# Mixture-of-experts feed-forward: weight loads with other contraction orders, bf16 transposes of x, and a finer last weight load

## The chip, the core and the metric

The kernel runs on one core of one Trainium2 chip. The metric is the device time of one execution in microseconds (us); lower is better. The core has TensorE (PE: matmuls, and the loads of their stationary operand, shown apart as PEld), VectorE (DVE), ScalarE (ACT), GpSimd (POOL), SyncE (SP) and 16 DMA engines that every queue shares.

## What is computed

```python
n_experts, capacity, hidden, expert_hidden = 8, 256, 512, 2048   # all inputs float32
def reference(x, w1, w2):          # x [8,256,512], w1 [8,512,2048], w2 [8,2048,512]
    h = np.matmul(x, w1)
    h = np.maximum(h, 0)
    return np.matmul(h, w2).astype(np.float32)
```

For each of eight experts a block of 256 tokens goes through two matrix products with a ReLU between them. Each expert has 4.19 MB of float32 in w1 and as much in w2, 0.52 MB of x and 0.52 MB of output: 67.1 MB of weights in all.

## The kernel before

The program is one loop over the experts, unrolled; a tile framework puts in the semaphores, and the instructions of each engine run in the order in which it placed them.

For one expert `e`:

- SP loads x (`x_sbuf`, L59): 128 tokens per half on the partitions, float32, in runs of 2 KB.
- PE transposes x in eight 128x128 float32 pieces (`xpsum`, L65), one PSUM buffer for all; ACT copies each piece to `xT_sbuf` as bf16 (L68) before the next can start.
- POOL loads w1 (`w1_sbuf`, L71) in one DMA that also casts to bf16. Partition `p` of chunk `ko` holds row `ko*128+p`; a row of w1 is one run of 2048 float32, 8 KB, and lands as 4 KB.
- PE computes h transposed: 64 matmuls of 256 columns (`h_psum`, L79), the stationary operand a 128x128 block of w1, unit step. ACT applies the ReLU (L87) and writes `hT_sbuf`. I call these 64 matmuls **the h part**, h(e).
- POOL loads w2 (`w2_c`, L102), again with the cast: a row is 512 float32, 2 KB, and lands as 1 KB. For the last expert this is cut into four DMAs, each into one of the four buffers of the pool.
- PE computes the output: 32 matmuls of 512 columns (`o_psum`, L113), first all 16 for the first 128 tokens, then 16 for the others; **the o part**, o(e). DVE copies each half to `out_sbuf` (L120) and SP stores it (L122), 0.5 MB in one DMA.

The weight pools have four buffers each, so POOL issues the loads of four experts at once and later ones as buffers come free; they run in the order of issue. The trace leaves digits out of names, so w1 and w2 appear there as `w_sbuf` and `w_c`.

Of the kernel before, what the change touches and what calls it, by code (L numbers as in the profile page):

```python
# [1 line left out]

# [5 lines left out]


@with_exitstack
def kernel(
    ctx: ExitStack,
    tc: tile.TileContext,
    x: bass.AP,
    w1: bass.AP,
    w2: bass.AP,
    out: bass.AP,
):
    nc = tc.nc  # L20
    P = 128
    n_experts, capacity, hidden = x.shape
    _, _, expert_hidden = w1.shape

    assert capacity % P == 0
    assert hidden % P == 0
    assert expert_hidden % P == 0

    M_CAP = capacity // P
    K1 = hidden // P  # L30
    K2 = expert_hidden // P
    assert K2 % 2 == 0

    fp32 = mybir.dt.float32
    bf16 = mybir.dt.bfloat16

    x_tiled = x.rearrange("e (mo p) k -> e p mo k", p=P)
    w1_tiled = w1.rearrange("e (ko p) n -> e p ko n", p=P)
    w2_tiled = w2.rearrange("e (ko p) n -> e p ko n", p=P)
    out_tiled = out.rearrange("e (mo p) k -> e p mo k", p=P)  # L40

    const = ctx.enter_context(tc.tile_pool(name="const", bufs=1))
    identity = const.tile([P, P], fp32)
    make_identity(nc, identity)

    x_pool = ctx.enter_context(tc.tile_pool(name="x_pool", bufs=3))
    xT_pool = ctx.enter_context(tc.tile_pool(name="xT_pool", bufs=3))
    w1_pool = ctx.enter_context(tc.tile_pool(name="w1_pool", bufs=4))
    w2_pool = ctx.enter_context(tc.tile_pool(name="w2_pool", bufs=4))
    hT_pool = ctx.enter_context(tc.tile_pool(name="hT_pool", bufs=3))  # L50
    out_pool = ctx.enter_context(tc.tile_pool(name="out_pool", bufs=3))

    psum_t = ctx.enter_context(tc.tile_pool(name="psum_t", bufs=1, space=bass.MemoryType.PSUM))
    psum_m1 = ctx.enter_context(tc.tile_pool(name="psum_m1", bufs=4, space=bass.MemoryType.PSUM))
    psum_m2 = ctx.enter_context(tc.tile_pool(name="psum_m2", bufs=3, space=bass.MemoryType.PSUM))

    for e in range(n_experts):
        x_sbuf = x_pool.tile([P, M_CAP, hidden], fp32, name="x_sbuf")
        nc.sync.dma_start(x_sbuf[:], x_tiled[e])  # L59

        xT_sbuf = xT_pool.tile([P, K1, capacity], bf16, name="xT_sbuf")
        for ko in range(K1):
            for mo in range(M_CAP):
                xpsum = psum_t.tile([P, P], fp32, name="xpsum")
                nc.tensor.transpose(  # L65
                    xpsum[:], x_sbuf[:, mo, ko * P:(ko + 1) * P], identity
                )
                nc.scalar.copy(xT_sbuf[:, ko, mo * P:(mo + 1) * P], xpsum[:])  # L68

        w1_sbuf = w1_pool.tile([P, K1, expert_hidden], bf16, name="w1_sbuf")  # L70
        nc.gpsimd.dma_start(w1_sbuf[:], w1_tiled[e])  # L71

        hT_sbuf = hT_pool.tile([P, K2, capacity], bf16, name="hT_sbuf")
        for mo_pair in range(K2 // 2):
            h_psum = psum_m1.tile([P, 2 * capacity], fp32, name="h_psum")
            for mo_sub2 in range(2):
                mo = mo_pair * 2 + mo_sub2
                for ko in range(K1):
                    nc.tensor.matmul(  # L79
                        h_psum[:, mo_sub2 * capacity:(mo_sub2 + 1) * capacity],  # L80
                        w1_sbuf[:, ko, mo * P:(mo + 1) * P],
                        xT_sbuf[:, ko, :],
                        start=(ko == 0),
                        stop=(ko == K1 - 1),
                    )
            mo = mo_pair * 2
            nc.scalar.activation(  # L87
                hT_sbuf[:, mo:mo + 2, :],
                h_psum[:],
                mybir.ActivationFunctionType.Relu,  # L90
            )

        last = (e == n_experts - 1)
        W2_CHUNK = 4 if last else 1
        k2_chunk = K2 // W2_CHUNK
        w2_sb = [None] * W2_CHUNK
        for ch in range(W2_CHUNK):
            w2_c = w2_pool.tile(
                [P, k2_chunk, hidden], bf16, name="w2_c", tag="w2",
                padded_shape=[P, K2, hidden],  # L100
            )
            nc.gpsimd.dma_start(  # L102
                w2_c[:], w2_tiled[e, :, ch * k2_chunk:(ch + 1) * k2_chunk, :]
            )
            w2_sb[ch] = w2_c

        out_sbuf = out_pool.tile([P, M_CAP, hidden], fp32, name="out_sbuf")
        for mo in range(M_CAP):
            o_psum = psum_m2.tile([P, hidden], fp32, name="o_psum")
            for ch in range(W2_CHUNK):  # L110
                for ko_sub in range(k2_chunk):
                    ko = ch * k2_chunk + ko_sub
                    nc.tensor.matmul(  # L113
                        o_psum[:],
                        hT_sbuf[:, ko, mo * P:(mo + 1) * P],
                        w2_sb[ch][:, ko_sub, :],
                        start=(ko == 0),
                        stop=(ko == K2 - 1),
                    )
            nc.vector.tensor_copy(out_sbuf[:, mo, :], o_psum[:])  # L120

        nc.sync.dma_start(out_tiled[e], out_sbuf[:])  # L122


# [1 line left out]
_INS = ['x', 'w1', 'w2']  # L126
_OUTS = [((8, 256, 512), 'float32')]


# [23 lines left out]
```

## Time and profile before

| | |
|---|---|
| median of 3 runs | 196.74 us (196.43 to 199.07) |
| span of the profiled execution, first to last instruction | 196.1 us (its own time is not recorded apart from the span) |
| PE busy, PEld busy | 142.4 us (73%), 86.1 us (44%) |
| ACT, DVE, POOL busy | 55.4, 11.1, 17.8 us |
| POOL's DMA queue (weights) | 33.56 MB written, 93.7% of 16 engines' span |
| the hardware queue (x and output) | 8.39 MB, 12.6% |

Bytes of a load are counted as written, after the cast, so 1 MB of weights in this table is 2 MB read. The PE times include its pipeline, so a high busy share is not the same as a full one.

### The profile page before, as it was taken

Reading aid. Unit: us, or ns where it says so; the run is one execution under the profiler, and the core shown is the slowest. Engines: PE = TensorE matmul, PEld = TensorE weight load, DVE = VectorE, ACT = ScalarE, POOL = GpSimd, SP = SyncE. Lnnn points to the kernel's source line nnn. Section 1 sums busy time; section 2 is a strip of 40 time slices with the busy share of each in tenths; the row PEclk is TensorE's granted clock in tenths of the full one; section 3 lists DMA queues with packets and bytes.
Section 4 is the critical chain, followed back from the end, with each engine's and each line's share of the span. In section 5 each row is a group of like instructions: output and inputs, shape, how many; then the busy total and the mean of one; then the engine's idle time right before and its main releaser. Section 6 shows DMA issues by size and latency. Waiting matters only on the chain.

```text
span 196.1 us, 1934 instructions
## 1 busy us (share of the span) xinstructions
PE 142.4 (73%) x832; PEld 86.1 (44%) x832; DVE 11.1 (6%) x16; ACT 55.4 (28%) x129; POOL 17.8 (9%) x25
## 2 busy tenths in 40 slices
PE   0102899869398785959489696958997695959990
PEld 0001485348133572337334374425853482437740
DVE  0000000200011000200001100110002000200011
ACT  2100262137101470026300363022721271024500
POOL 8900001200102000020100100010001000010000
PEclk9999999999979999999958999995899999996999
DMA  5999999999999999999999999999999999999702
GB/s 206 226 236 203 200 232 242 208 243 252 225 216 205 250 255 218 214 221 249 244 216 208 208 259 253 216 206 253 212 218 208 248 212 219 215 216 237 121 0 107
DMA packets 25143, 42.05 MB, mean 214 GB/s; under 512 B 560, under 2 KB 16944, under 8 KB 25136
## 3 DMA queue, kind: packets, MB, share of 16 engines
q0 software_dynamic: 20784, 33.56, 93.7%
q1 hardware_dynamic: 4352, 8.39, 12.6%
q8 instruction: 6, 0.10, 0.2%
q14 instruction: 1, 0.01, 0.0%
HBM read 71.30 MB, written 4.19 MB: 385 GB/s over the span
## 4 chain that ended last, share of the span: by engine, by line
PE 58%; DMA 25%; another core or an unknown queue 7%; ACT 4%; POOL 2%; issue 2%; DVE 0%; POOLq 0%; ACTq 0%
PE o_psum L113 27%; DMA w_c<-in_w_dram 25%; PE h_psum L79 24%; PE xpsum L65 7%; ACT xT_sbuf L68 4%; POOL w_sbuf L71 1%; POOL w_c L102 1%; DVE out_sbuf L120 0%; POOL identity masks.py:199 0%; POOL identity masks.py:197 0%; POOLq masks.py:199 0%; ACTq L68 0%; POOLq L137 0%
## 5 line engine op out<-in xcount | busy, mean ns | idle before, releaser
L79 PE MATMUL h_psum<-xT_sbuf,w_sbuf 128*128 128x256 bf16 x512 | 67.3, 288 | 20.0 <-DMA w_sbuf<-in_w_dram 17.1
L113 PE MATMUL o_psum<-w_c,hT_sbuf 128*128 128x512 bf16 x256 | 61.3, 401 | 13.4 <-DMA w_c<-in_w_dram 13.4
L79 PEld LDWEIGHTS <-w_sbuf 128*128 128x128 bf16 x512 | 53.8, 106 | 30.5 <-DMA w_sbuf<-in_w_dram 18.4
L68 ACT CAST xT_sbuf<-xpsum 128x128 bf16<-128x128 f32 x64 | 17.0, 266 | 111.0 <-PE xpsum L65 111.0
L113 PEld LDWEIGHTS <-hT_sbuf 128*128 128x128 bf16 x256 | 25.9, 103 | 46.5 <-DMA w_c<-in_w_dram 11.1
L87 ACT ACTIVATE hT_sbuf<-h_psum 128x512 bf16<-128x512 f32 x64 | 37.1, 597 | 18.3 <-PE h_psum L79 18.1
L65 PE MATMUL xpsum<-identity,x_sbuf 128*128 128x128 f32 x64 | 22.0, 344 | 15.9 <-ACT xT_sbuf L68 11.3
L65 PEld LDWEIGHTS xpsum<-identity,x_sbuf 128*128 128x128 f32 x64 | 9.8, 153 | 28.0 <-ACT xT_sbuf L68 22.3
L120 DVE COPY out_sbuf<-o_psum 128x512 f32<-128x512 f32 x16 | 11.1, 692 | 181.4 <-PE o_psum L113 181.4
L102 POOL DMA_DIRECT2D w_c<-in_w_dram x11 | 11.2, 1014 | 100.2 <-PE xpsum L65 100.2
L71 POOL DMA_DIRECT2D w_sbuf<-in_w_dram x8 | 6.2, 779 | 53.6 <-PE h_psum L79 53.3
L68 ACT ACT_TABLE_LOAD x1 | 1.3, 1283 | 0.7 <-PEq L137 0.7
masks.py:199 POOL TENSOR_SCALAR_AFFINE_SELECT identity<-identity 128x128 f32<-128x128 f32 x1 | 0.3, 304 | 0.1
masks.py:197 POOL MEMSET identity<- 128x128 f32 x1 | 0.2, 204 | 0.3 <-POOLq L137 0.3
L137 POOL MEMSET const-float32-0.0<- 128x1 f32 x1 | 0.1, 98 | 0.2 <-issue 0.2
L137 POOL MEMSET const-bfloat16-1.0<- 128x1 bf16 x1 | 0.1, 101 | 0.0
L137 POOL MEMSET const-uint8-127<- 128x1 uint8 x1 | 0.1, 101 | 0.0
L137 POOL MEMSET const-float32-1.0<- 128x1 f32 x1 | 0.1, 98 | 0.0
## 6 DMA issues: line engine op xcount, KB each, us to landing
w_sbuf<-in_w_dram POOLq DMA_DIRECT2D x8, 2048.0 KB, 77.7
w_c<-in_w_dram POOLq DMA_DIRECT2D x7, 2048.0 KB, 80.7
x_sbuf<-in_x_dram SPq DMA_DIRECT2D x8, 512.0 KB, 7.7
out_dram<-out_sbuf SPq DMA_DIRECT2D x8, 512.0 KB, 6.9
w_c<-in_w_dram POOLq DMA_DIRECT2D x4, 512.0 KB, 42.1
```

Source lines behind the costliest of these rows:

```text
L65: nc.tensor.transpose(xpsum[:], x_sbuf[:, mo, ko * P:(ko + 1) * P], identity)
L68: nc.scalar.copy(xT_sbuf[:, ko, mo * P:(mo + 1) * P], xpsum[:])
L71: nc.gpsimd.dma_start(w1_sbuf[:], w1_tiled[e])
L79: nc.tensor.matmul(h_psum[:, mo_sub2 * capacity:(mo_sub2 + 1) * capacity], w1_sbuf[:, ko, mo * P:(mo + 1) * P], xT_sbuf[:, ko, :], start=( ...
L87: nc.scalar.activation(hT_sbuf[:, mo:mo + 2, :], h_psum[:], mybir.ActivationFunctionType.Relu,)
L102: nc.gpsimd.dma_start(w2_c[:], w2_tiled[e, :, ch * k2_chunk:(ch + 1) * k2_chunk, :])
L113: nc.tensor.matmul(o_psum[:], hT_sbuf[:, ko, mo * P:(mo + 1) * P], w2_sb[ch][:, ko_sub, :], start=(ko == 0), stop=(ko == K2 - 1),)
L120: nc.vector.tensor_copy(out_sbuf[:, mo, :], o_psum[:])
L137: nc = _bacc.Bacc("TRN2", target_bir_lowering=False, num_devices=1)
```

## The change

The same sums are made in another order of the contraction axis, so that memory is read in other runs.

- w1: partition `p` holds rows `4p` to `4p+3` of one expert, one run of 32 KB (16 KB as bf16). x must then be contracted in the same order: chunk `ko` takes the columns `4p+ko` of x, picked by a step of four elements.
- w2: partition `p` of block `b` holds rows `512b+4p` to `512b+4p+3`, one run of 8 KB (4 KB as bf16). h must come out in that order: the stationary block of w1 now takes every fourth column, a step of four bf16 elements (8 bytes).
- x and the output: partition `p` holds tokens `2p` and `2p+1`, runs of 4 KB.
- x is cast to bf16 by DVE (L101), transposed in bf16 by eight matmuls into one PSUM tile (L105), and copied out by one DVE copy of 1024 elements (L107). ACT no longer takes part in it.
- The last expert's w2 comes in six DMAs (4, 4, 4, 2, 1, 1 chunks of 128 rows) into buffers of their own (L82), its o part goes chunk by chunk over both halves of the tokens, and each half is copied (one by DVE, one by ACT) and stored (SP, ACT) by itself.
- POOL issues w1 of expert 0 ahead of the identity matrix.

```diff
-    x_tiled = x.rearrange("e (mo p) k -> e p mo k", p=P)
-    w1_tiled = w1.rearrange("e (ko p) n -> e p ko n", p=P)
-    w2_tiled = w2.rearrange("e (ko p) n -> e p ko n", p=P)
-    out_tiled = out.rearrange("e (mo p) k -> e p mo k", p=P)
+    x_v = x.rearrange("e (p mo) k -> e p (mo k)", mo=MC)
+    out_v = out.rearrange("e (p mo) k -> e p (mo k)", mo=MC)
+    w1_v = w1.rearrange("e (p ko) n -> e p (ko n)", ko=K1)
+    w2_v = w2.rearrange("e (b p j) n -> e p b (j n)", p=P, j=J)
...
+            pieces = [4, 4, 4, 2, 1, 1]
+            k = 0
+            for i, n in enumerate(pieces):
+                b, j = divmod(k, J)
+                c = w2_pool.tile([P, n * H], BF16, name=f"w2_last{i}", bufs=1)
+                nc.gpsimd.dma_start(c[:], w2_v[e, :, b, j * H:(j + n) * H])
...
+    load_x(0)
+    load_x(1)
+    load_w1(0)
+    make_identity(nc, identity)
+    load_w2(0)
...
+        xb = xb_pool.tile([P, MC, P, K1], BF16, name="xb")
+        nc.vector.tensor_copy(xb[:].rearrange("p m q k -> p (m q k)"), xs[e][:])
+        xt_ps = psum_t.tile([P, K1, MC, P], BF16, name="xt_ps")
         for ko in range(K1):
-            for mo in range(M_CAP):
-                xpsum = psum_t.tile([P, P], fp32, name="xpsum")
-                nc.tensor.transpose(
-                    xpsum[:], x_sbuf[:, mo, ko * P:(ko + 1) * P], identity
-                )
-                nc.scalar.copy(xT_sbuf[:, ko, mo * P:(mo + 1) * P], xpsum[:])
+            for mo in range(MC):
+                nc.tensor.transpose(xt_ps[:, ko, mo, :], xb[:, mo, :, ko], identity[:])
+        xT = xT_pool.tile([P, K1, C], BF16, name="xT")
+        nc.vector.tensor_copy(
+            xT[:].rearrange("p k c -> p (k c)"),
+            xt_ps[:].rearrange("p k m q -> p (k m q)"),
+        )
...
+        w1_r = w1s[e][:].rearrange("p (ko b q j) -> p ko b q j", ko=K1, b=NB, j=J)
...
-                        w1_sbuf[:, ko, mo * P:(mo + 1) * P],
-                        xT_sbuf[:, ko, :],
+                        w1_r[:, ko, b, :, j],
+                        xT[:, ko, :],
...
+        if last:
+            order = [(k, m) for k in range(K2) for m in range(MC)]
+        else:
+            order = [(k, m) for m in range(MC) for k in range(K2)]
...
+                if last and m == 1:
+                    nc.scalar.copy(out_sb[:, m, :], o_ps[m][:])
+                else:
+                    nc.vector.tensor_copy(out_sb[:, m, :], o_ps[m][:])
+                if last:
+                    eng = nc.scalar if m == 1 else nc.sync
+                    eng.dma_start(out_v[e, :, m * H:(m + 1) * H], out_sb[:, m, :])
```

Where the order of instructions changes, three places matter. The first is PE between o(6) and h(7). Before, the last output matmul is followed by three transposes, then by the first h matmuls with the other transposes between them; each `Activation` wait is on ACT's copy of the transpose ahead.

```order
L113 MATMUL o_psum<-w_c,hT_sbuf 128x512
L65 MATMUL xpsum<-identity,x_sbuf 128x128 [waits DMAHW3_49]
L65 MATMUL xpsum<-identity,x_sbuf 128x128 [waits Activation_49] x2
L79 LDWEIGHTS w_sbuf [waits DMASW6_49]
L79 MATMUL h_psum<-xT_sbuf,w_sbuf 128x256 [waits PE_49]
```

The same place after; seven pairs like the first two L105 rows stand ahead of this, and the one `DVE` wait is on the copy of all eight transposes.

```order
L105 LDWEIGHTS xb
L105 MATMUL xt_ps<-identity,xb 128x128
L119 LDWEIGHTS w_sb [waits DMASW6_49]
L119 MATMUL h_ps<-xT,w_sb 128x256 [waits DVE_49]
L119 LDWEIGHTS w_sb
```

All transposes have moved ahead of the first h matmul, and nothing stands between h matmuls any more. On DVE, after, the copy of the transposes for expert 7 (L107) stands behind both output copies of expert 6 (L151) and ahead of the one that remains on DVE for expert 7:

```order
L151 COPY out_sb<-o_ps 128x512 [waits DMAHW3_49,PE_49]
L151 COPY out_sb<-o_ps 128x512 [waits PE_49]
L107 COPY xT<-xt_ps 128x1024 [waits DVE_49,PE_49]
L151 COPY out_sb<-o_ps 128x512 [waits DMAHW4_49,PE_49]
```

So a DVE copy of expert 6's second half can stand between the transposes and their copy. The third place is POOL's last loads, before (buffer numbers shown; `PE` is the wait for a buffer to come free, `DMASW` for an earlier load on the same semaphore):

```order
L71 DMA w1_sbuf_1167<-in_w1_dram 128x4x2048 [waits DMASW6_49,PE_49]
L102 DMA w2_c_1250<-in_w2_dram 128x4x512 [waits DMASW7_49,PE_49]
L102 DMA w2_c_1252<-in_w2_dram 128x4x512 [waits DMASW1_49,DMASW0_49,PE_49]
L102 DMA w2_c_1254<-in_w2_dram 128x4x512 [waits DMASW3_49,PE_49]
L102 DMA w2_c_1256<-in_w2_dram 128x4x512 [waits DMASW5_49,DMASW2_49,PE_49]
```

and after:

```order
L64 DMA w1_sb_929<-in_w1_dram 128x8192 [waits DMASW6_49,PE_49]
L82 DMA w2_last0_932<-in_w2_dram 128x2048 [waits DMASW7_49]
L82 DMA w2_last1_934<-in_w2_dram 128x2048 [waits DMASW0_49]
L82 DMA w2_last2_936<-in_w2_dram 128x2048 [waits DMASW1_49]
L82 DMA w2_last3_938<-in_w2_dram 128x1024 [waits DMASW2_49]
L82 DMA w2_last4_940<-in_w2_dram 128x512 [waits DMASW3_49]
```

The last pieces wait for no buffer any more, only for loads of experts 3 to 6.

## Rows read from the trace of the kernel before

**Rows 1.** The page: the span in 40 slices, DMA share and GB/s written.

```profile
DMA  5999999999999999999999999999999999999702
GB/s 206 226 236 203 200 232 242 208 243 252 225 216 205 250 255 218 214 221 249 244 216 208 208 259 253 216 206 253 212 218 208 248 212 219 215 216 237 121 0 107
```

**Rows 2.** Timeline of PE, 60 to 196 us: start, duration, what, idle before and releaser.

```profile
75.79 7.08 PE L113 MATMUL o_psum<-w_c,hT_sbuf 128*128 128x512 bf16 x32 [2.99 <-DMA w_c<-in_w_dram]
85.55 0.61 PE L79 MATMUL h_psum<-xT_sbuf,w_sbuf 128*128 128x256 bf16 x4 [1.14 <-DMA w_sbuf<-in_w_dram]
...
98.61 10.05 PE L113 MATMUL o_psum<-w_c,hT_sbuf 128*128 128x512 bf16 x32 [3.41 <-DMA w_c<-in_w_dram]
...
121.43 7.08 PE L113 MATMUL o_psum<-w_c,hT_sbuf 128*128 128x512 bf16 x32 [1.63 <-DMA w_c<-in_w_dram]
131.20 0.61 PE L79 MATMUL h_psum<-xT_sbuf,w_sbuf 128*128 128x256 bf16 x4 [1.15 <-DMA w_sbuf<-in_w_dram]
...
152.55 0.61 PE L79 MATMUL h_psum<-xT_sbuf,w_sbuf 128*128 128x256 bf16 x4 [0.89 <-DMA w_sbuf<-in_w_dram]
...
156.35 5.84 PE L79 MATMUL h_psum<-xT_sbuf,w_sbuf 128*128 128x256 bf16 x52 [0.35 <-ACT xT_sbuf L68]
164.17 7.08 PE L113 MATMUL o_psum<-w_c,hT_sbuf 128*128 128x512 bf16 x32 [1.98 <-DMA w_c<-in_w_dram]
```

**Rows 3.** Timeline of all engines from 165 us on: the last expert.

```profile
171.55 0.74 POOL L102 DMA_DIRECT2D w_c<-in_w_dram  x1 [20.39 <-PE xpsum L65]
...
173.90 0.61 PE L79 MATMUL h_psum<-xT_sbuf,w_sbuf 128*128 128x256 bf16 x4 [1.11 <-DMA w_sbuf<-in_w_dram]
...
178.24 6.56 PE L79 MATMUL h_psum<-xT_sbuf,w_sbuf 128*128 128x256 bf16 x52 [0.35 <-ACT xT_sbuf L68]
...
184.63 7.07 PE L113 MATMUL o_psum<-w_c,hT_sbuf 128*128 128x512 bf16 x32
...
191.74 0.69 DVE L120 COPY out_sbuf<-o_psum 128x512 f32<-128x512 f32 x1 [2.76 <-PE o_psum L113]
```

**Rows 4.** DMA view, 171 to 196 us: issue to landing of the last w2 load.

```profile
w_c<-in_w_dram POOLq DMA_DIRECT2D x1, 512.0 KB, 13.9
```

**Rows 5.** DMA view, 158 to 161 us: only w2 moves.

```profile
DMA packets 610, 0.62 MB, mean 208 GB/s; under 512 B 0, under 2 KB 610, under 8 KB 610
```

**Rows 6.** DMA view, 166 to 172 us: w1 moves, and one instruction fetch.

```profile
DMA packets 312, 1.29 MB, mean 215 GB/s; under 512 B 0, under 2 KB 0, under 8 KB 311
```

**Rows 7.** DMA view, 185 to 196.1 us in 40 slices: the last store, GB/s.

```profile
GB/s 7 0 0 0 0 0 0 0 0 0 0 0 0 0 0 0 0 0 0 0 0 0 0 0 0 0 0 0 0 0 339 391 376 369 384 30 0 0 0 0
```

**Rows 8.** Instructions by line: count, busy us, mean ns, idle before.

```profile
L79 PEld LDWEIGHTS <-w_sbuf 128*128 128x128 bf16 x512 | 53.8, 106 | 30.5 <-DMA w_sbuf<-in_w_dram 18.4 <-issue 4.5
...
L65 PEld LDWEIGHTS xpsum<-identity,x_sbuf 128*128 128x128 f32 x64 | 9.8, 153 | 28.0 <-ACT xT_sbuf L68 22.3 <-issue 4.4
```

**Rows 9.** Stretches: busy us by engine, granted PE clock, DMA share, GB/s.

```profile
98.00:102.00 4.00, 3.39 (x8) 1.19 (x9) 0.00 (x0) 0.00 (x0) 0.00 (x0) 0.50 1.06 215
176.00:180.00 4.00, 3.30 (x16) 2.34 (x17) 0.00 (x0) 1.23 (x4) 0.00 (x0) 0.57 1.17 255
```

**Rows 10.** Timeline, first 30 us.

```profile
0.74 23.10 SPq L59 DMA_DIRECT2D x_sbuf<-in_x_dram  x4
1.27 0.87 POOL L71 DMA_DIRECT2D w_sbuf<-in_w_dram  x1 [0.33 <-issue]
...
18.61 0.82 PE L79 MATMUL h_psum<-xT_sbuf,w_sbuf 128*128 128x256 bf16 x3 [12.08 <-DMA w_sbuf<-in_w_dram]
```

More of the change, by code (lines that the diff above doesn't have):

```diff
@@ L8 @@
 from concourse.masks import make_identity
+FP32 = mybir.dt.float32
+BF16 = mybir.dt.bfloat16
+J = 4
 @with_exitstack
@@ L21 @@
     P = 128
[L22 to L35, printed above, removed]
-    x_tiled = x.rearrange("e (mo p) k -> e p mo k", p=P)
-    w1_tiled = w1.rearrange("e (ko p) n -> e p ko n", p=P)
-    w2_tiled = w2.rearrange("e (ko p) n -> e p ko n", p=P)
@@ L40 @@
-    out_tiled = out.rearrange("e (mo p) k -> e p mo k", p=P)
+    E, C, H = x.shape
+    F = w1.shape[2]
+    MC = C // P
+    K1 = H // P
+    K2 = F // P
+    NB = K2 // J
+    x_v = x.rearrange("e (p mo) k -> e p (mo k)", mo=MC)
+    out_v = out.rearrange("e (p mo) k -> e p (mo k)", mo=MC)
+    w1_v = w1.rearrange("e (p ko) n -> e p (ko n)", ko=K1)
+    w2_v = w2.rearrange("e (b p j) n -> e p b (j n)", p=P, j=J)
     const = ctx.enter_context(tc.tile_pool(name="const", bufs=1))
-    identity = const.tile([P, P], fp32)
@@ L51 @@
     out_pool = ctx.enter_context(tc.tile_pool(name="out_pool", bufs=3))
     psum_t = ctx.enter_context(tc.tile_pool(name="psum_t", bufs=1, space=bass.MemoryType.PSUM))
[L54 to L61, printed above, removed]
-        for ko in range(K1):
-            for mo in range(M_CAP):
-                xpsum = psum_t.tile([P, P], fp32, name="xpsum")
-                nc.tensor.transpose(
-                    xpsum[:], x_sbuf[:, mo, ko * P:(ko + 1) * P], identity
-                )
-                nc.scalar.copy(xT_sbuf[:, ko, mo * P:(mo + 1) * P], xpsum[:])
[L70 to L77, printed above, removed]
@@ new lines, with load_x, load_w1 @@
+    psum_h = ctx.enter_context(tc.tile_pool(name="psum_h", bufs=4, space=bass.MemoryType.PSUM))
+    psum_o = ctx.enter_context(tc.tile_pool(name="psum_o", bufs=3, space=bass.MemoryType.PSUM))
+    identity = const.tile([P, P], BF16, name="identity")
+    xs, w1s, w2s = {}, {}, {}
+    def load_x(e):
+        t = x_pool.tile([P, MC * H], FP32, name="x_sb")
+        nc.sync.dma_start(t[:], x_v[e])
+        xs[e] = t
+    def load_w1(e):
+        t = w1_pool.tile([P, K1 * F], BF16, name="w1_sb")
+        nc.gpsimd.dma_start(t[:], w1_v[e])
+        w1s[e] = t
@@ new lines, in load_w2 @@
+    def load_w2(e):
+        t = w2_pool.tile([P, NB, J * H], BF16, name="w2_sb")
+        w2s[e] = []
+        if e < E - 1:
+            nc.gpsimd.dma_start(t[:], w2_v[e])
+            for b in range(NB):
+                for j in range(J):
+                    w2s[e].append(t[:, b, j * H:(j + 1) * H])
+        else:
[5 more added lines that the diff above has]
+                nc.gpsimd.dma_start(c[:], w2_v[e, :, b, j * H:(j + n) * H])
+                for q in range(n):
+                    w2s[e].append(c[:, q * H:(q + 1) * H])
+                k += n
@@ new lines @@
+    load_x(0)
[3 more added lines that the diff above has]
+    load_w2(0)
+    for e in range(E):
+        if e + 1 < E:
+            load_w1(e + 1)
+            load_w2(e + 1)
+        if e + 2 < E:
+            load_x(e + 2)
+        xb = xb_pool.tile([P, MC, P, K1], BF16, name="xb")
+        nc.vector.tensor_copy(xb[:].rearrange("p m q k -> p (m q k)"), xs[e][:])
+        xt_ps = psum_t.tile([P, K1, MC, P], BF16, name="xt_ps")
+        for ko in range(K1):
+            for mo in range(MC):
[6 more added lines that the diff above has]
+        w1_r = w1s[e][:].rearrange("p (ko b q j) -> p ko b q j", ko=K1, b=NB, j=J)
+        hT = hT_pool.tile([P, K2, C], BF16, name="hT")
+        for pr in range(K2 // 2):
+            h_ps = psum_h.tile([P, 2, C], FP32, name="h_ps")
+            for s in range(2):
+                b, j = divmod(pr * 2 + s, J)
@@ L85 @@
                     )
-            mo = mo_pair * 2
             nc.scalar.activation(
-                hT_sbuf[:, mo:mo + 2, :],
-                h_psum[:],
+                hT[:, pr * 2:pr * 2 + 2, :].rearrange("p a c -> p (a c)"),
+                h_ps[:].rearrange("p a c -> p (a c)"),
                 mybir.ActivationFunctionType.Relu,
             )
[L93 to L100, printed above, removed]
-            )
[L102 to L120, printed above, removed]
@@ L122 @@
-        nc.sync.dma_start(out_tiled[e], out_sbuf[:])
+        last = e == E - 1
+        out_sb = out_pool.tile([P, MC, H], FP32, name="out_sb")
+        o_ps = [psum_o.tile([P, H], FP32, name="o_ps") for _ in range(MC)]
+        if last:
+            order = [(k, m) for k in range(K2) for m in range(MC)]
+        else:
+            order = [(k, m) for m in range(MC) for k in range(K2)]
+        for k, m in order:
+            nc.tensor.matmul(
+                o_ps[m][:],
+                hT[:, k, m * P:(m + 1) * P],
+                w2s[e][k],
+                start=(k == 0),
+                stop=(k == K2 - 1),
+            )
+            if k == K2 - 1:
+                if last and m == 1:
+                    nc.scalar.copy(out_sb[:, m, :], o_ps[m][:])
+                else:
+                    nc.vector.tensor_copy(out_sb[:, m, :], o_ps[m][:])
+                if last:
+                    eng = nc.scalar if m == 1 else nc.sync
+                    eng.dma_start(out_v[e, :, m * H:(m + 1) * H], out_sb[:, m, :])
@@ L126 @@
+        if not last:
+            nc.sync.dma_start(out_v[e], out_sb[:].rearrange("p m h -> p (m h)"))
 _INS = ['x', 'w1', 'w2']
```

8 lines of the change are left out of this document (4 added, 4 removed).

## The prediction

> **What bounds the kernel now.** I read the slices first. The DMA engines are full from the second slice to the 37th, at 200 to 259 GB/s written [rows 1]: the weights stream without a break, and only the last three slices, some 14 us, are something else. Then the waits of PE. It waits for w2 ahead of o parts and for w1 ahead of h parts, in nearly every expert [rows 2], so PE follows the stream. The last stage is different. w1 of expert 7 has landed at 173.90. From there PE works without a wait for DMA until 191.74 [rows 3]. The last quarter of w2, issued at 171.55, lands 13.9 us later, at 185.45 [rows 3, 4], and o(7) takes its chunks in order, so it is not waited for. So the time is: the stream up to the landing of w1(7), T = 173.90; then PE, 17.84 us; then copy, store and end, 196.1 - 191.74 = 4.36 us. The median, 196.74, lies 0.64 above the span; I add that to what I get. A measurement of this kernel can tell about 2% from no change, that is 192.8 and 200.7.
>
> **The stream, part by part.** The landings seen by PE [rows 2, 3] give w1 alone: 75.79 to 85.55, 121.43 to 131.20, 164.17 to 173.90, so 9.76, 9.77 and 9.73, mean 9.75 us for 2.097 MB written, 215 GB/s; the stretch with only w1 shows the same 215 [rows 6]. w2 with one store beside it took 152.55 to 164.17, 11.62 us. w2 alone runs at 208 GB/s [rows 5], so 10.08 us of it; or, the other way, a store alone runs at some 370 GB/s [rows 7], 1.4 us for its 0.524 MB, which leaves 10.22. So a w1 packet of 8 KB read costs 16 x 4096 B / 215 = 304.8 ns on one engine and a w2 packet of 2 KB read 16 x 1024 B / 208 = 78.8 ns; four of these are 315. The run length is worth 3 to 4.5%, no more.
>
> - *w2 from 2 KB to 8 KB runs* is the run of w1 now. It takes w1's 9.75: 0.33 to 0.47 us less each, I take 0.40. Seven of them lie ahead of T: 2.8 us (2.3 to 3.3). The eighth lies beside PE's work.
> - *w1 from 8 KB to 32 KB runs* has no row. A straight line through the two packets leaves 3.5 ns fixed per packet; a packet of 16 KB written would be 1209 ns, 217 GB/s, 0.09 us less for each of eight: 0.7. The other end is nothing; a loss is a rival below. I take 0.35.
> - *x and output from 2 KB to 4 KB runs*: 8 packets of 16 saved on each engine, by the same 3.5 ns 0.03 us, for eight loads and six stores ahead of T: 0 to 0.4, I take 0.2.
> - *w1(0) ahead of the identity*: its issue now starts at 1.27, x's at 0.74 [rows 10]. 0.53 at most; but three x loads, 1.57 MB, fill the engines meanwhile (at the store's 370 GB/s 4.2 us). 0 to 0.5, I take 0.2.
>
> Sum 3.55 (2.3 to 4.9): T = 170.35. The buffers don't enter: four for each weight before and after, and the stream had no gap [rows 1]. The last pieces of w2 no longer wait for a buffer and come ahead of time. x goes onto SP's queue before the stores, two experts early, so longer packets of weights between its own can delay it without harm.
>
> **After T.** [...] After, the transposes are ahead of T. The h part at full clock goes at 5.84 / 52 = 0.112 us a matmul [rows 2]: 64 take 7.19. With the o part 14.13. The end of w2 doesn't hold it up: w2 and the store of expert 6 end at T + 9.75 + 1.4 = T + 11.2, while the last pair of matmuls is due at T + 13.7; with the finer pieces the earlier chunks come in step.
>
> What can make h(7) late is the way from o(6) to the transposed x. The eight transposes have half the columns of an h matmul and cost at most 0.11 each, 0.9; the DVE copy of 1024 elements is twice the 0.69 of 512 [rows 3], 1.4; the output copy queued ahead of it runs beside the transposes. So xT is ready 2.3 us after o(6). w2(6) lands at T - 9.75. If o(6) takes 7.08, xT is there at T - 0.4. If it takes 10.05, as after the wait of 3.41 us [rows 2], xT comes at T + 2.6. The wait will often be longer than now: h ends 7.2 after its w1, w2 lands 11.2 after it, 4.0 us. But an h part that starts 2.6 late waits only 1.4 for its w2, so late and punctual experts should alternate. I charge a third of 2.6, 0.9: PE needs 15.0 (14.1 to 17.1) after T, ends at 185.35. The end is left at 4.36: the two half stores move the same 0.5 MB, 1.4 us of it, and their copies run side by side. Some 0.4 could go. Span 189.7, time **190.3 us**.
>
> ACT gives up 17 us of copies and DVE takes eight casts and eight copies of 1.4 us, 22 us on an engine that was busy 11 of 196. Both hide behind the stream except as just counted.
>
> **Rivals.**
>
> *1. Strided weight loads are slow, and PE becomes the bound.* The h part's stationary block now has a step of 8 bytes; no row before has any step. Contiguous, the load takes 106 ns at 256 bytes per partition, the float32 one 153 at 512 [rows 8]. Drawn on along the 1024 bytes that 128 columns now span, it is 106 + 3 x 47 = 247 ns; the lower end is 106, hidden behind the matmul. PE per expert would be 64 loads plus 7.1 plus 2.3, against a stream of 20.9 (2 x 9.75 + 1.4). So it decides from 180 ns; at 203 the time is 18.6 + 8 x (13.0 + 9.4) - 2.3 + 5.0 = 200.5, the bound of slower; at 247 it is 223 us. I take the near end, since two neighbouring columns still lie within 16 bytes and the block is no larger: 12% for this rival, 10% above 200.7. [...]
>
> *2. Run length isn't what slows w2.* Then the stream keeps its rates and only the start and PE's end are gained: 173.7 + 15.0 + 5.0 = 193.7, within 2%. Against it stand the equal landings of three w1 loads; for it, that rows 5 and 6 differ by 3% only, near what the edges of such stretches can make. 11%. If 32 KB runs are even slower, every 1% on the weights costs 1.5 us; 6 to 7% would eat the whole gain. Nothing shows it: 3%, half of it slower.
>
> *3. The faster PE waits longer and pays in clock.* At 98.61 an o part after a wait of 3.41 us took 10.05 instead of 7.08, with 0.50 granted between 98 and 102 [rows 2, 9]; after 2.99 it took 7.08. [...] 10%. [...]
>
> *4. Everything goes right*: the far end of each term, T = 169.0, 14.1 after it, 0.4 off the end: 187.7.
>
> **How the numbers follow.** The forecast's own case with rival 4, 187 to 192.8: 64%. Rivals 2 and 3, 193 to 196: 21%, and of the loads' middle prices (110 to 200 ns, which cost up to 64 x 0.09 = 5.8 at the end) 2%. Slower than 200.7: 10% from rival 1, with the loss in 2 and what I don't see 13%. So faster 0.65, same 0.22, slower 0.13. The range reaches over rivals 2 and 3, 186.8 to 196.5, and leaves out rival 1 and little else.
>
> **What would show it.** w1 and w2 both landing some 9.7 us after one another, GB/s near 216 in stretches of either; w1(7) at 170 to 171; h parts of 7.2 us with loads near 100 ns; PE's end 14 to 16 us after w1(7). I am wrong if LDWEIGHTS of w1 shows 180 ns or more and PE stops waiting for DMA, if w1(7) still lands near 174, or if h(7) starts late at half clock.

## The result, and the profile after

The changed kernel takes **190.02 us** (median of 4 runs, 189.92 to 191.25), the kernel before 197.91 (4 runs, 196.43 to 199.21): ratio 0.963, 95% interval 0.955 to 0.970. A second set of runs gave 189.96 and a ratio of 0.957 (0.951 to 0.962). Beside the later experiments the kernel before had medians of 198.7 to 199.1. The span of the profiled execution is 188.0 us, its own time 190.07.

From the page after: the busy time of the engines, then the 40 slices that answer to [rows 1].

```profile
PE 131.7 (70%) x832; PEld 88.7 (47%) x832; DVE 20.6 (11%) x31; ACT 40.1 (21%) x66; POOL 13.7 (7%) x27
...
PEclk9999997899958999589999998599987999699999
DMA  7999999999999999999999999989999999999912
GB/s 248 230 214 256 274 274 230 223 195 236 274 243 223 187 262 281 221 200 213 264 237 209 205 266 244 216 186 218 262 234 223 191 265 229 213 207 238 227 18 112
DMA packets 8167, 42.05 MB, mean 224 GB/s; under 512 B 608, under 2 KB 864, under 8 KB 7136
```

The DMA engines move the same bytes (42.05 MB) and are full as before, now up to the last two slices, where before it was the last three. The timeline of PE after, from 96 us on, answers to [rows 2, 3]: start, duration, what, idle time before it and what ended that. I call the start of a matmul that waited for a load the landing of this load.

```profile
96.81 7.07 PE L140 MATMUL o_ps<-w_sb,hT 128*128 128x512 bf16 x32 [2.48 <-DMA w_sb<-in_w_dram]
...
106.54 7.18 PE L119 MATMUL h_ps<-xT,w_sb 128*128 128x256 bf16 x64 [2.22 <-DMA w_sb<-in_w_dram]
117.62 9.54 PE L140 MATMUL o_ps<-w_sb,hT 128*128 128x512 bf16 x32 [3.90 <-DMA w_sb<-in_w_dram]
...
138.41 8.75 PE L140 MATMUL o_ps<-w_sb,hT 128*128 128x512 bf16 x32 [2.72 <-DMA w_sb<-in_w_dram]
147.00 0.61 PE L105 MATMUL xt_ps<-identity,xb 128*128 128x128 bf16 x8
148.54 7.15 PE L119 MATMUL h_ps<-xT,w_sb 128*128 128x256 bf16 x64 [0.93 <-DVE xT L107]
159.23 8.75 PE L140 MATMUL o_ps<-w_sb,hT 128*128 128x512 bf16 x32 [3.54 <-DMA w_sb<-in_w_dram]
167.82 0.61 PE L105 MATMUL xt_ps<-identity,xb 128*128 128x128 bf16 x8
169.36 7.18 PE L119 MATMUL h_ps<-xT,w_sb 128*128 128x256 bf16 x64 [0.93 <-DVE xT L107]
176.38 7.07 PE L140 MATMUL o_ps<-w_last,hT 128*128 128x512 bf16 x32
```

Two landings in a row of the same kind give the pace of the stream: w2(5) at 138.41 and w2(6) at 159.23 are 20.82 us apart, where before w1(6) at 152.55 and w1(7) at 173.90 were 21.35 apart. w2(6) comes 4.94 us earlier than before, at 159.23 instead of 164.17. After it the profile shows no wait of PE for DMA: o(6), transposes, copy, h(7) and o(7) follow one another up to 183.49, where ACT takes over, then 4.51 us to the end. The single steps stand in the chain of waits, here its last 29 us:

```profile
159.23 8.77 PE o_ps L140 x32
...
168.63 0.69 DVE xT L107
...
169.36 7.18 PE h_ps L119 x64
176.54 6.92 PE o_ps L140 x32
...
183.49 0.59 ACT out_sb L149
```

No DMA is in it. The granted clock of PE in two stretches of o(6) goes with its 8.75 us in place of 7.07; it is the number behind the busy times of the five engines:

```profile
159.00:163.00 4.00, 3.77 (x12) 1.42 (x12) 0.00 (x0) 0.00 (x0) 0.00 (x0) 0.65 0.94 201
163.00:168.00 5.00, 5.00 (x26) 2.32 (x25) 0.69 (x1) 0.00 (x0) 0.00 (x0) 0.94 0.95 202
```

The first stretch, with 0.65 granted, follows a wait of 3.54 us; in the second 0.94 was granted. Instructions by line, the loads of w1's blocks, answer to [rows 8]:

```profile
L119 PEld LDWEIGHTS <-w_sb 128*128 128x128 bf16 x512 | 56.3, 114 | 20.7 <-DMA w_sb<-in_w_dram 16.4 <-issue 3.2
```

### The profile page after: what moved, and what is told of

Read it like the earlier page. It is cut to its first block, busy times and chain, and to the rows that moved or that the text cites. A ratio compares the mean times of both kernels' runs of the same rounds, so it can differ in the third digit from the quotient of the medians.

```text
span 188.0 us, 1894 instructions
## 1 busy us (share of the span) xinstructions
PE 131.7 (70%) x832; PEld 88.7 (47%) x832; DVE 20.6 (11%) x31; ACT 40.1 (21%) x66; POOL 13.7 (7%) x27
## 2 busy tenths in 40 slices
DMA packets 8167, 42.05 MB, mean 224 GB/s; under 512 B 608, under 2 KB 864, under 8 KB 7136
## 4 chain that ended last, share of the span: by engine, by line
PE 55%; DMA 26%; another core or an unknown queue 10%; issue 2%; DVE 2%; POOL 1%; ACT 0%; DVEq 0%; POOLq 0%
PE o_ps L140 32%; DMA w_sb<-in_w_dram 26%; PE h_ps L119 23%; DVE xT L107 2%; POOL w_sb L64 1%; POOL w_sb L72 0%; ACT out_sb L149 0%; PE xt_ps L105 0%; POOL identity masks.py:199 0%; POOL identity masks.py:197 0%; DVE out_sb L151 0%; DVEq L151 0%; POOLq masks.py:199 0%; DVEq L101 0%
## 5 line engine op out<-in xcount | busy, mean ns | idle before, releaser
L140 PE MATMUL o_ps<-w_sb,hT 128*128 128x512 bf16 x224 | 61.8, 444 | 28.0 <-DMA w_sb<-in_w_dram 28.0
L119 PE MATMUL h_ps<-xT,w_sb 128*128 128x256 bf16 x512 | 58.8, 277 | 18.8 <-DMA w_sb<-in_w_dram 13.2
L126 ACT ACTIVATE hT<-h_ps 128x512 bf16<-128x512 f32 x64 | 38.2, 597 | 136.9 <-PE h_ps L119 136.9
L119 PEld LDWEIGHTS <-w_sb 128*128 128x128 bf16 x512 | 56.3, 114 | 20.7 <-DMA w_sb<-in_w_dram 16.4
L140 PEld LDWEIGHTS <-hT 128*128 128x128 bf16 x256 | 27.9, 109 | 67.0 <-issue 45.8
L151 DVE COPY out_sb<-o_ps 128x512 f32<-128x512 f32 x15 | 10.4, 692 | 148.1 <-PE o_ps L140 148.1
L105 PE MATMUL xt_ps<-identity,xb 128*128 128x128 bf16 x64 | 5.3, 231 | 5.0 <-DVE xb L101 5.0
L72 POOL DMA_DIRECT2D w_sb<-in_w_dram x7 | 5.3, 752 | 41.4 <-PE o_ps L140 41.4
L64 POOL DMA_DIRECT2D w_sb<-in_w_dram x8 | 4.7, 584 | 43.0 <-PE h_ps L119 42.2
L105 PEld LDWEIGHTS <-xb 128*128 128x128 bf16 x64 | 4.7, 118 | 6.5 <-DVE xb L101 5.0
L101 DVE CAST xb<-x_sb 128x1024 bf16<-128x1024 f32 x8 | 5.9, 735 | 15.2 <-DMA x_sb<-in_x_dram 15.2
L140 PE MATMUL o_ps<-w_last,hT 128*128 128x512 bf16 x32 | 7.1, 379 | 0.0
L82 POOL DMA_DIRECT2D w_last<-in_w_dram x6 | 3.2, 532 | 50.5 <-DMA w_sb<-in_w_dram 50.5
L107 DVE COPY xT<-xt_ps 128x1024 bf16<-128x1024 bf16 x8 | 5.4, 680 | 0.0
```

The costliest lines, as they stand in the source:

```text
L64: nc.gpsimd.dma_start(t[:], w1_v[e])
L72: nc.gpsimd.dma_start(t[:], w2_v[e])
L82: nc.gpsimd.dma_start(c[:], w2_v[e, :, b, j * H:(j + n) * H])
L101: nc.vector.tensor_copy(xb[:].rearrange("p m q k -> p (m q k)"), xs[e][:])
L105: nc.tensor.transpose(xt_ps[:, ko, mo, :], xb[:, mo, :, ko], identity[:])
L107: nc.vector.tensor_copy(xT[:].rearrange("p k c -> p (k c)"), xt_ps[:].rearrange("p k m q -> p (k m q)"),)
```

## The experiments

Unless it is said otherwise each is an edit of the changed kernel. Ratios are to the kernel before, which ran beside each. The changed kernel took 190.0 in both of its sets of runs, so I compare with 190.0 where it didn't run beside an experiment; a difference of some tenths of a us then shows nothing.

**Run lengths, one at a time.** Three kernels undo one run length each, a fourth gives w2 alone its long runs in the kernel before.

`e1_w2_short`:

```diff
-    w2_v = w2.rearrange("e (b p j) n -> e p b (j n)", p=P, j=J)
+    w2_v = w2.rearrange("e (b j p) n -> e p b j n", p=P, j=J)
...
-                        w1_r[:, ko, b, :, j],
+                        w1_r[:, ko, b, j, :],
```

> The changed kernel with w2 back in runs of 2 KB (and w1's stationary blocks contiguous again, which this order needs). Theory A, run length: w2 with a store beside it goes from 11.1 back to 11.6 us, seven times ahead of the landing of w1(7): that lands at 172.4 instead of 168.9, the time is about 193.5 against 190.0. Rival B, the stream gained from something else (start, x, queue order): w2 keeps 11.1, time 190.0. The loads of w1 blocks go from 113 to 98 ns and change nothing in either.

Measured: 193.3 us (192.45 to 193.62), ratio to before 0.972 (0.967 to 0.978).

`e2_w1_short`:

```diff
-    w1_v = w1.rearrange("e (p ko) n -> e p (ko n)", ko=K1)
+    w1_v = w1.rearrange("e (ko p) n -> e p ko n", p=P)
...
-                nc.tensor.transpose(xt_ps[:, ko, mo, :], xb[:, mo, :, ko], identity[:])
+                nc.tensor.transpose(xt_ps[:, ko, mo, :], xb[:, mo, ko, :], identity[:])
```

> The changed kernel with w1 back in runs of 8 KB, x contracted in contiguous columns. Theory A, the gain ends at 8 KB: w1 goes from 9.68 to 9.75 us, 0.5 us over eight, time 190.5. Rival C, the 32 KB runs carry what the stream gained beyond w2 (w1(7) landed 5.0 us earlier, of which seven w2 and w1 at 0.55 explain 3.9): time 191.5 or more, and the first w1 lands at 18.6 instead of 17.0.

Measured: 191.6 us (190.44 to 192.41), ratio 0.964 (0.958 to 0.970).

`e8_xo_short`:

```diff
-    x_v = x.rearrange("e (p mo) k -> e p (mo k)", mo=MC)
-    out_v = out.rearrange("e (p mo) k -> e p (mo k)", mo=MC)
+    x_v = x.rearrange("e (mo p) k -> e p mo k", mo=MC)
+    out_v = out.rearrange("e (mo p) k -> e p mo k", mo=MC)
...
```

> The changed kernel with x and output in runs of 2 KB. Theory A: 0.2 to 0.4 us in all, time 190.3. Rival D, the 1.1 us of the stream that w1 and w2 leave unexplained come from longer packets of x and output: time 191 to 191.5, and w1(7) lands at 170.

Measured: 192.1 us (191.92 to 192.87), ratio 0.968 (0.962 to 0.974).

`e6_before_w2_long`, an edit of the kernel before:

```diff
-    w2_tiled = w2.rearrange("e (ko p) n -> e p ko n", p=P)
+    w2_tiled = w2.rearrange("e (b p j) n -> e p b (j n)", p=P, j=4)
...
-                        w1_sbuf[:, ko, mo * P:(mo + 1) * P],
+                        w1_sbuf[:, ko, :].rearrange("p (b q j) -> p b q j", b=4, j=4)[:, mo // 4, :, mo % 4],
...
```

> The kernel before with w2 alone in runs of 8 KB, and so with stationary blocks of w1 at a step of 8 bytes. Theory A: w2 with a store from 11.6 to 11.1 us, w1(7) lands 3 to 3.5 us earlier (170.6), PE's 17.8 us after that stay: the time falls by 3 to 3.5, ratio 0.983. Rival B: no change. Rival E, strided loads cost something when transposes stand between: the h part grows beyond 11 us and the gain is less than 2.

Measured: 196.2 us (195.15 to 197.26) against 199.1, ratio 0.9875 (0.980 to 0.995). The medians differ by 2.9, the ratio is worth 2.5 us; theory A had 3 to 3.5.

The landings say more than times that differ by 1%. The rows are of the timeline of PE: the last in each is the first output matmul of expert 6, released by w2(6), and ahead of it stands an earlier landing. In e1, w2(5) and w2(6):

```profile
140.71 7.07 PE L140 MATMUL o_ps<-w_sb,hT 128*128 128x512 bf16 x31 [2.67 <-DMA w_sb<-in_w_dram]
...
161.88 0.58 PE L140 MATMUL o_ps<-w_sb,hT 128*128 128x512 bf16 x1 [4.33 <-DMA w_sb<-in_w_dram]
```

In e2, w2(3) and w2(6):

```profile
97.51 0.58 PE L140 MATMUL o_ps<-w_sb,hT 128*128 128x512 bf16 x1 [3.95 <-DMA w_sb<-in_w_dram]
...
160.20 0.59 PE L140 MATMUL o_ps<-w_sb,hT 128*128 128x512 bf16 x1 [3.98 <-DMA w_sb<-in_w_dram]
```

In e8, again w2(3) and w2(6):

```profile
97.56 0.58 PE L140 MATMUL o_ps<-w_sb,hT 128*128 128x512 bf16 x1 [4.15 <-DMA w_sb<-in_w_dram]
...
160.38 0.58 PE L140 MATMUL o_ps<-w_sb,hT 128*128 128x512 bf16 x1 [4.08 <-DMA w_sb<-in_w_dram]
```

In e6, w1(6), w2(6) and w1(7):

```profile
151.19 0.63 PE L79 MATMUL h_psum<-xT_sbuf,w_sbuf 128*128 128x256 bf16 x4 [0.35 <-DMA w_sbuf<-in_w_dram]
...
162.48 7.08 PE L113 MATMUL o_psum<-w_c,hT_sbuf 128*128 128x512 bf16 x31 [1.63 <-DMA w_c<-in_w_dram]
...
172.20 0.95 PE L79 MATMUL h_psum<-xT_sbuf,w_sbuf 128*128 128x256 bf16 x4 [1.11 <-DMA w_sbuf<-in_w_dram]
```

Against 159.23, w2's short runs cost 2.65, w1's 0.97 and x's with the output's 1.15 us. In six further kernels that load up to w2(6) as the changed one does, this landing lies between 158.90 and 159.30, so these are outside its scatter. The sum is 4.77, and the kernel before is 4.94 later, so the three run lengths, undone one at a time, account for nearly all of what the stream gained. No run undoes all three together, and of the kernel before there is one profile.

Rival B (the gain comes from something else) is out: e1 gave back 2.65 us. Theory A and rival C of e2 are both off: A had 0.5 us and 190.5, C had all that w2 leaves, 191.5 or more, and the first w1 at 18.6. The time of 191.6 is C's, but by the landing the 32 KB runs carry 0.97 of the 2.29 us that w2 leaves, and x with the output 1.15. For these D was right; its time, at most 191.5, was passed by 0.6.

The spans grew by more than the landings did, by 3.1, 1.6 and 1.9 us in e1, e2 and e8. The rest is o(6): from its start to the transposes it took 9.1, 9.3 and 9.4 us there, 8.6 in the changed kernel.

In e6 the landing moved by only 1.69 and not by 2.65. The pace of the stream shows where the difference isn't. Between the last two landings of one kind e6 took 21.01, 0.34 less than the kernel before; e1 took 21.17, 0.35 more than the changed kernel. So once all x is loaded a w2 gains the same in both kernels, and what differs lies earlier, while x moves too. The same holds of e2 and e8: at w2(3) they are already 0.70 and 0.75 late (96.81 after), and lose only 0.27 and 0.40 in the three periods from there to w2(6). In e6 the h part of expert 6 took 9.67 us from its first matmul to its last, 9.64 before; the pages have 9 tenths of the clock or more in all its slices, in both. h(7) took 11.8 instead of 10.7: in e6 the page has 6 tenths in two slices, from 171.1 to 180.8 us, before in one, from 176.5 to 181.4. So rival E, a cost of the strided loads themselves, is not seen.

In e1 the blocks of w1 are contiguous again; their loads by line:

```profile
L119 PEld LDWEIGHTS <-w_sb 128*128 128x128 bf16 x512 | 50.5, 99 | 25.9 <-DMA w_sb<-in_w_dram 16.2 <-issue 3.0
```

So a load with the step of 8 bytes took 15 ns longer (114 against 99). It is hidden: h(7) took 6.98 us in e1, from 172.53 to 179.51, and 7.02 in the changed kernel.

**The handover and the last loads.** The handover is the way from o(6) over the transposes to h(7). All but e5 ran beside the changed kernel.

`a_after_again`: no edit.

> The changed kernel itself, beside the three that follow, so that they can be compared on one chip: a ratio near 0.963 to the kernel before.

Measured: 189.96 us (189.78 to 190.88), ratio 0.957 (0.951 to 0.962). In its profile w2(6) lands at 159.03, 0.2 earlier, but o(6) took 9.87 instead of 8.75, and the span is 188.9 instead of 188.0.

`e3_old_transposes`:

```diff
-        nc.vector.tensor_copy(xb[:].rearrange("p m q k -> p (m q k)"), xs[e][:])
...
+                xpsum = psum_t.tile([P, P], FP32, name="xpsum")
+                nc.tensor.transpose(xpsum[:], xf[:, mo, :, ko], identity[:])
+                nc.scalar.copy(xT[:, ko, mo * P:(mo + 1) * P], xpsum[:])
...
```

> The changed kernel with the transposes as before: eight in float32 (here at a step of four elements), one PSUM buffer, ACT copies. Theory A, the handover from o(6) to h(7) is on the path: PE needs some 27.5 us from the landing of w2(6) to its end, as before, instead of 24.3, so the time grows by 3 to 190 + 3 = 193. Rival B, the stream alone decides: no change. The landings of the weights stay within 0.5 us in both.

Measured: 193.6 us (192.19 to 194.18), ratio 0.974 (0.965 to 0.982). The timeline of PE in e3:

```profile
159.09 7.08 PE L136 MATMUL o_ps<-w_sb,hT 128*128 128x512 bf16 x32 [1.23 <-DMA w_sb<-in_w_dram]
...
168.75 0.63 PE L115 MATMUL h_ps<-xT,w_sb 128*128 128x256 bf16 x4 [0.93 <-DMA w_sb<-in_w_dram]
...
173.19 6.69 PE L115 MATMUL h_ps<-xT,w_sb 128*128 128x256 bf16 x52 [0.35 <-ACT xT L106]
179.71 7.07 PE L136 MATMUL o_ps<-w_last,hT 128*128 128x512 bf16 x32
```

w2(6) lands as in the changed kernel to 0.14 us, and o(6) is even faster by 1.7 (its wait was 1.23 us, and 1.00 of the clock was granted from 159 to 166 us). h(7) too starts earlier, at 168.75, when w1(7) lands. Yet o(7) starts 3.3 us later than at 176.38: with the transposes and ACT's copies between its matmuls h(7) took 10.96 us instead of 7.02. Part of it goes with the clock: its last 52 matmuls took 6.69, where the page has 7 tenths granted in the slice from 172.2 to 177.0 us; before, with 1.00 granted from 152.5 to 173.9, they took 5.84 [rows 2]. So the old transposes are on the path, as theory A has it.

`e4_w2last_one`:

```diff
-            pieces = [4, 4, 4, 2, 1, 1]
+            pieces = [16]
...
```

> The changed kernel with the last w2 in one DMA instead of six. Theory A, the pieces let o(7) start at 176.4 while w2 still moves: in one DMA w2(7) lands at some 168.9 + 11.1 = 180.0, o(7) waits 3.6 us, time 193.7. Rival B, PE is late anyway and the pieces give nothing: 190.

Measured: 194.9 us (193.59 to 195.35), ratio 0.980 (0.973 to 0.986). PE in e4:

```profile
179.72 8.74 PE L140 MATMUL o_ps<-w_last,hT 128*128 128x512 bf16 x32 [3.48 <-DMA w_last<-in_w_dram]
```

w2(7) lands at 179.72, 0.3 from the 180.0 worked out. The wait is 3.5, as expected; that o(7) then takes 1.7 more, with 0.59 of the clock granted from 179 to 183 us, was not.

`e5_w2last_halves`: four pieces, o(7) half by half.

```diff
-            pieces = [4, 4, 4, 2, 1, 1]
+            pieces = [4, 4, 4, 4]
...
-            order = [(k, m) for k in range(K2) for m in range(MC)]
+            order = [(k, m) for m in range(MC) for k in range(K2)]
```

> The changed kernel with the last w2 in four DMAs and o(7) half by half, as before, in place of six DMAs and chunk by chunk. Theory: the first half needs the last quarter at 176.4 + 2.6 = 179.0, it lands at 180.0, so 1.0 us more: 191.0. Rival: the six pieces matter for more than that, 192 or above; or for nothing, 190.0.

Measured: 190.35 us (190.24 to 190.53), ratio 0.959 (0.953 to 0.965). In e5 h(7) waits for w1(7), and o(7) for its last quarter:

```profile
169.23 7.18 PE L119 MATMUL h_ps<-xT,w_sb 128*128 128x256 bf16 x64 [1.37 <-DMA w_sb<-in_w_dram]
176.25 2.75 PE L140 MATMUL o_ps<-w_last,hT 128*128 128x512 bf16 x12
179.82 4.48 PE L140 MATMUL o_ps<-w_last,hT 128*128 128x512 bf16 x20 [0.82 <-DMA w_last<-in_w_dram]
```

That the last w2 comes in pieces is worth 5 us against one DMA (e4), which the kernel before, with its four, had already. Six in place of four, with the new order, end PE 0.8 us earlier; the span differs by 0.3 and the time by 0.35, too little to be told from nothing without the changed kernel beside it.

`e7_w1last_split`:

```diff
...
+            w1_c = w1.rearrange("e (p ko) n -> e p ko n", ko=K1)
+            r = t[:].rearrange("p (b ko f) -> p b ko f", b=NB, ko=K1)
+            for b in range(NB):
+                nc.gpsimd.dma_start(r[:, b], w1_c[e, :, :, b * J * P:(b + 1) * J * P])
...
```

> The changed kernel with w1 of the last expert in four DMAs of 512 columns each (runs of 2 KB), so that h(7) can start on the first quarter, 7 us before the last. Theory F: PE is the bound already from the landing of w2(6) on, since o(6), eight transposes, h(7) and o(7) follow on one another almost without a gap; h(7) can't start before o(6) is done at 168 and the copy of xT at 169.3: time the same, 189.5 to 190.5. Rival A, the reading of the prediction, PE's last work starts with the landing of w1(7): h(7) overlaps it, PE ends 4 us or more earlier, time 186.

Measured: 189.5 us (189.32 to 189.76), 0.4 less than the changed kernel beside it, ratio 0.954 (0.949 to 0.959). PE in e7:

```profile
159.30 8.47 PE L149 MATMUL o_ps<-w_sb,hT 128*128 128x512 bf16 x32 [3.66 <-DMA w_sb<-in_w_dram]
167.61 0.61 PE L115 MATMUL xt_ps<-identity,xb 128*128 128x128 bf16 x8
169.15 7.15 PE L128 MATMUL h_ps<-xT,w_sb 128*128 128x256 bf16 x64 [0.93 <-DVE xT L117]
```

h(7) is still released by the copy of xT, at 169.15. Splitting w1(7) doesn't bring it forward, since PE is at o(6) and its transposes until then. Theory F holds, and rival A's 4 us are not there; what the 0.4 us come from is not shown (o(6) took 8.47 in this profile, 8.75 and 9.87 in the two of the changed kernel).

**What theory F suggests.** If PE has no slack from w2(6) on, its work has to be moved ahead. These three ran beside one another, not beside the changed kernel.

`e9_early_transposes`: the block from L100 to L110 becomes a function that is called for expert e+1 ahead of o(e).

```diff
...
+        if e + 1 < E:
+            prep(e + 1)
         last = e == E - 1
```

> The changed kernel with the transposes of expert e+1 moved ahead of o(e), into PE's wait for w2(e). Theory F (PE is the bound from the landing of w2(6)): h(7) starts when o(6) is done and w1(7) is there, at about 168.9 instead of 169.4 to 170.3, so 0.4 to 1.4 us less: 189.0. Rival A, the stream alone sets it: no change, 190.0.

`e11_early_w2six`: the same, and w2(6) in four DMAs with its o part chunk by chunk.

```diff
+                if e == E - 2:
+                    nc.gpsimd.dma_start(t[:, b, :], w2_v[e, :, b, :])
...
-        if last:
+        if e >= E - 2:
             order = [(k, m) for k in range(K2) for m in range(MC)]
```

> As the run with early transposes, and w2(6) in four DMAs, o(6) chunk by chunk over both halves, so that o(6) ends some 2 us after the landing of w2(6) instead of 8.7. [...]

`e10_all_three`: all of e11, and w1(7) in four DMAs as in e7.

> Early transposes, w2(6) in four and w1(7) in four column pieces. Theory F: now nothing of PE's work is late, h(7) follows the quarters of w1(7), o(7) the pieces of w2(7), and the end is the landing of w2(7) at 180.0 plus the last pair of matmuls, 0.5, and the end, 4.5: span 185, time 187.0; 188 if the clock falls in the waits. Rival A: 186 or less, since the split takes 4 us off by itself. Rival G, the shorter runs of w1(7) and the waits on more semaphores cost what is gained: 190.

Measured: e9 189.45 us (189.28 to 191.43), ratio 0.957 (0.948 to 0.967); e11 191.7 (190.88 to 192.31), ratio 0.965 (0.958 to 0.972); e10 **188.04** (187.98 to 188.21), ratio 0.947 (0.941 to 0.953). PE in e9, where h(7) now waits for w1(7) and so shows its landing:

```profile
158.90 8.56 PE L150 MATMUL o_ps<-w_sb,hT 128*128 128x512 bf16 x32 [3.52 <-DMA w_sb<-in_w_dram]
168.57 7.18 PE L127 MATMUL h_ps<-xT,w_sb 128*128 128x256 bf16 x64 [1.10 <-DMA w_sb<-in_w_dram]
```

PE in e11:

```profile
156.77 7.07 PE L154 MATMUL o_ps<-w_sb,hT 128*128 128x512 bf16 x32
168.51 8.83 PE L131 MATMUL h_ps<-xT,w_sb 128*128 128x256 bf16 x64 [4.67 <-DMA w_sb<-in_w_dram]
```

PE in e10:

```profile
155.47 7.07 PE L163 MATMUL o_ps<-w_sb,hT 128*128 128x512 bf16 x32
162.37 3.80 PE L140 MATMUL h_ps<-xT,w_sb 128*128 128x256 bf16 x32
...
170.71 1.94 PE L140 MATMUL h_ps<-xT,w_sb 128*128 128x256 bf16 x16 [2.00 <-DMA w_sb<-in_w_dram]
173.10 1.89 PE L163 MATMUL o_ps<-w_last,hT 128*128 128x512 bf16 x8 [0.46 <-DMA w_last<-in_w_dram]
...
178.02 3.61 PE L163 MATMUL o_ps<-w_last,hT 128*128 128x512 bf16 x16 [0.57 <-DMA w_last<-in_w_dram]
```

In e9 w1(7) lands 9.67 after w2(6). h(7) starts 0.8 earlier than in the changed kernel and is now released by w1(7), as theory F has it; the time, 0.5 below 190.0 where 1.0 was expected, can't be told from rival A's 190.0. In e11 o(6) starts at 156.77 without a wait, and what it gains turns into a wait of 4.67 ahead of h(7), which starts no earlier than in e9 and takes 8.83 in place of 7.18, with 0.51 of the clock granted from 168.5 to 172; e11 is 2.3 us slower than e9. I had put it at 189.0 with the clock held, up to 3 us more without, an estimate; h(7) shows 1.65 us. In e10 PE follows the stream to its last piece, and the time is 1% below the changed kernel's. It is 1.0 above the 187.0 expected: the last quarter of w1(7) came at 170.7 instead of 168.9. The clock is not the reason: 1.00 was granted from 159 to 168 us, and the page has 9 tenths or more in every slice from 144 us on. The runs of w1(7) are of 2 KB, and the store of expert 6, issued earlier, now lies beside it; what either of the two costs wasn't tried.

## Why the prediction was right, and where a size was off

*The bound.* Right in its order: the stream up to w1(7), then PE to the end without a wait for w2(7), which in e4 landed 20.8 us after w2(6), where the forecast's terms give 20.9. But two paths meet at h(7), and they are almost level. In the changed kernel h(7) waits for xT, and so for o(6) and w2(6); splitting w1(7) doesn't help (e7), and without the transposes behind o(6) h(7) starts when w1(7) lands (e9). In e5 it is w1(7) that comes last, 10.22 after w2(6). The prediction had the late h(7) in a charge of 0.9 us. Its picture of it was wrong: late and punctual experts don't alternate; of h(1) to h(7) only h(4), at 106.54, began on its w1, the other six on xT.

*The stream.* T was put at 170.35; with the 9.67 of e9 behind 159.23 it was 168.9 (with the 10.22 of e5 it can't have been: h(7) began at 169.36). w2 with a store beside it took 11.08 (106.54 to 117.62), as a w1 of 9.75 and 1.4 for the store make 11.15. The 0.40 per w2 was about right: e1 gives 2.65 over the seven up to w2(6), 0.38 each. Two terms were too small, each measured beyond its own bound: w1's 32 KB runs, put at 0.35 (at most 0.7), cost 0.97 to undo, and x with the output, put at 0.2 (at most 0.4), 1.15. I had priced only the fixed 3.5 ns of a packet. For w1 alone that fits: from w2(3) on e2 loses 0.09 a period, the price that I had worked out. What it leaves out came earlier, while x moved beside the weights. How short and long packets delay one another there, no run shows. The 0.2 for w1(0) ahead of the identity didn't come from the issue, which starts at 1.23 instead of 1.27.

*After T.* The span fell by 8.1 us: 5.0 up to T and 3.25 from there to PE's end, while the end grew by 0.15. 15.0 was forecast for PE, 183.49 - 168.9 = 14.6 measured: 14.13 of matmuls as worked out, h(7) late by 0.46. The 6.94 for the o part in it is the time from the end of h(7) before, 184.80, to 191.74 [rows 3]; after, the chain has 6.92. xT was there 1.4 us after o(6), not 2.3: the copy of 1024 bf16 elements took 0.68, not the 1.4 I drew from 0.69 for 512 float32. o(6) took 8.75, between the two cases. The end took 4.51, not 4.36. e3 shows what the new transposes are worth, 3.7 us in the time. The losses of e1, e2, e8 and e3 in time, 10.7 us together, are more than the whole gain, so they can't be added up.

*What lies around the span.* 0.64 was wrong. The changed kernel has 190.07 for a span of 188.0, 2.07 more; a run of the kernel before beside e3 has 196.48 for 194.7. The median I added it from was of other executions than the profile's. So the span was forecast 1.7 too long and its surroundings 1.4 too short; that 190.3 lies so near to 190.0 is luck to the extent of these 1.4.

*Rivals.* 1 falls: 114 ns a load, far from 180, hidden. The pace of the h part is the one worked out, 7.18 us for 64 matmuls against 7.19; the load itself isn't quite that of a contiguous block, 114 ns against 99. My reason for the near end, two neighbouring columns within 16 bytes, was not shown: no run has w1's blocks at any step but 8 bytes, or contiguous. 2 falls by e1. 3 is real, and paid where it costs little: of the seven o parts after a wait, the six with waits of 2.72 to 5.36 us took 8.5 to 9.9 us, the one with 2.48 took 7.07. Those up to o(5) end while the stream still runs, and of the 1.7 that o(6) took longer at most the 0.46 by which h(7) is late can lie on the path, since w1(7) isn't there before. Where o(6) takes longer still, it shows: 9.87 in a_after_again, and a span longer by 0.9. The length of the wait alone doesn't tell: 8.75 followed 2.72 here, 7.08 followed 2.99 before [rows 2]. The price that 193 to 196 has for an h(7) both late and at a lowered clock is shown by no run: in the changed kernel h(7) took 7.18 us, with 1.00 granted from 168 to 177 us; in e11, where it wasn't late, 8.83, with 0.51 from 168.5 to 172. 4 came for the stream, whose T of 168.9 is its 169.0, and not for what follows.

## What to carry to other kernels

In this full stream longer runs raised the rate by a few per cent (two landings of a kind 20.82 us apart instead of 21.35), and the runs of the small transfers beside it counted too (1.15 us up to w2(6), e8). Read the last stage backwards to the last moment at which the busy engine waited, and ask by how much: here two paths ended within half a us. A load that is split behind that moment gives next to nothing (0.4 us in e7), and a load split so that its work is done sooner can lose, if the next work still waits for its own load (e11, 2.3 us behind e9). Take the time around the span from the same execution as the span.

## What the runs showed of the hardware that was not expected

The length of w1's runs changed which load landed first. In the first 25 us after, DVE waits 10.66 us for the third x, issued with the first two (timeline of all engines):

```profile
17.04 8.17 PE L119 MATMUL h_ps<-xT,w_sb 128*128 128x256 bf16 x59 [11.00 <-DMA w_sb<-in_w_dram]
17.57 0.69 DVE L101 CAST xb<-x_sb 128x1024 bf16<-128x1024 f32 x1 [10.66 <-DMA x_sb<-in_x_dram]
```

With w1 in runs of 8 KB (e2) DVE has the third x at 10.32, and w1(0) comes at 21.77 instead of 17.04 (timeline of PE):

```profile
21.77 8.77 PE L119 MATMUL h_ps<-xT,w_sb 128*128 128x256 bf16 x64 [15.87 <-DMA w_sb<-in_w_dram]
```

By w2(6) only 0.97 us of these 4.73 are left: the order changed more than the sum. And DVE copied 1024 bf16 elements out of PSUM in 0.68 us, as fast as 512 float32 in 0.69 (instructions by line, after):

```profile
L151 DVE COPY out_sb<-o_ps 128x512 f32<-128x512 f32 x15 | 10.4, 692 | 148.1 <-PE o_ps L140 148.1
...
L107 DVE COPY xT<-xt_ps 128x1024 bf16<-128x1024 bf16 x8 | 5.4, 680 | 0.0
```
